# Interleaving attention with the projections in a hybrid decoder block, with the rotary swap moved from TensorE to DMA

## The chip, the cores and the metric

The kernel runs on the eight cores of one Trainium2 chip. Each core computes half of one sequence (2048 tokens of its own, with up to 2048 tokens of history before them) and no core speaks to another. The metric is the device time of the slowest core, in microseconds (us).

Engines: PE is TensorE (PEld its weight loads), ACT is ScalarE, DVE is VectorE, POOL is GpSimd, SP is SyncE. A "q" behind the name means the engine's instruction queue, which also issues DMAs. L306 means line 306 of the program; where a helper function issues every matmul, all matmuls carry one line.

## The reference, cut to what matters

```python
u = rms_norm(h, norm_mix)
q, k, v, z, g_att, g_pool = split(u @ w_in)         # 24 heads of 64; 512 pool channels; 2 gates of 1024
q, k = partial_rope(q), partial_rope(k)             # first 16 dims of each head
att    = dilated_attention(q, k, v)                 # three groups (window, dilation): (128,1) (512,4) (2048,16)
pooled = multiscale_pool(z) @ w_pool_group * scale  # trailing means over 2, 4, 8, 16 tokens, minus the token
merged = sigmoid(g_att) * (att @ w_att_branch) + sigmoid(g_pool) * (pooled @ w_pool_branch)
h = h + merged @ w_out
f = rms_norm(h, norm_ffn)
h = h + (silu(f @ w_ffn_gate) * (f @ w_ffn_up)) @ w_ffn_down
return rms_norm(h, norm_final)
```

Every query sees 129 keys of each group, at distances that are multiples of the dilation. A core works on the heads in four strips; a strip is two heads of each of the three groups. The softmax is taken without subtracting the maximum: two accumulators per head slot collect numerators and denominators of the three groups, and one division per strip ends it ("the norm" of a strip below).

## The kernel before

It is hand-scheduled with explicit semaphores and goes through the stages one by one. x is stored transposed, so tokens are columns. A strip first projects q, k and v of all three groups ("units" of eight matmuls of 512 columns), with a permutation matmul for the rotary partner of each q/k unit:

```python
# one q/k unit
for c in range(8):
    t = mm(psq[:, 0:N], wpv[:, c, wcol:wcol + 128], rhs_fn(c), c == 0, c == 7, after=[t_wp, psq_free[i]])
t_raw = act(qrawv[i], psq, AF.Copy, ...)                 # bf16 copy for the permutation
t_t1  = tt(t1v[i], psq, cosv, ALU.mult, ...)
# one unit later (do_perm)
t_p  = mm(pss, prmv, qrawv[i], True, True, ...)          # 8 rows up, 8 rows down
t_t2 = tt(t2v[i], pss, sinv, ALU.mult, ...)
t_o  = tt(dst, shp(t1v[i]), shp(t2v[i]), ALU.add, ...)
```

Only when all of it is done (`t_Pdone`) does the strip's attention begin, one 128-query block at a time: four score matmuls of 64 rows, an exponential of 512 columns, a mask, four value matmuls. A full barrier stands behind the norm of x, behind the last strip, behind the pooling mixer and behind the gated merge.

```python
for ti, tile in enumerate(tiles):                        # 48 blocks per strip
    ...  mm(ps[:, c0_:c0_ + 128], ktv[...], q, True, True, after=list(sfree[i2]) + t_Pdone)
    t_e = act(ptv[i4], ps2, AF.Exp, after=[t, ptfree[i4]], scale=0.125)
    t_m = tt(ptv[i4], ptv[i4], mv, ALU.mult, after=[t_e, t_msk])
    ...                                                  # value matmuls four blocks later
    # group with dilation 4: output columns slice(r4, 512, 4), that is with a step of 4 in PSUM
P.barrier()                                              # behind the last strip
```

The softmax here doesn't subtract the row's maximum and nothing guards it: scores larger than these inputs give would overflow.

Of the kernel before, what the change touches and what calls it, by code (L numbers as in the profile page):

```python
# [6 lines left out]
F32 = mybir.dt.float32  # L7
# [8 lines left out]
NJ = 22  # L16
EPS = 1e-6
GROUPS = ((128, 1), (512, 4), (2048, 16))
NBLK = (17, 20, 32)
KT_OFF = (0, 2176, 4736)  # L20
VS_OFF = (0, 17 * 192, 37 * 192)

NW = 52512
UT_H, UT_O, ATT = 0, 8192, 16384
CST, MSK, PRM, ONE = 20480, 20608, 21120, 21184
R = 21504
TAB, QT, KT, VS, ACC, WP, PT, QRAW, T12 = R, 25600, 28672, 33088, 39712, 43808, 48416, 49440, 49952
XS, SQ, RS = 25600, 33792, 35840
POOLT, MERGED, TMPB = 29696, 33792, 41984
ACTT, RS2 = 8192, 19456  # L30
FT, WGU, WD, SQ2, SIL, OST = 29696, 33792, 39936, 46080, 48128, 49152

class Tok:
    __slots__ = ("sem", "val")

    def __init__(self, sem, val):
        self.sem, self.val = sem, val

class DSem:
    def __init__(self, sem):  # L40
        self.sem, self.cnt = sem, 0

class Prog:
    ENGS = ("pe", "act", "dve", "pool", "sp")
    CE = ("pe", "act", "dve")

    def __init__(self, nc, es):
        self.nc, self.es = nc, es
        self.ops = {e: [] for e in self.ENGS}
        self.esem = {e: es.enter_context(nc.semaphore("es_" + e)) for e in self.CE}  # L50
        self.ecnt = {e: 0 for e in self.CE}
        self.seen = {e: {} for e in self.ENGS}
        self.nsem = 0
        self.dma_out = []

    def dsem(self):
        self.nsem += 1
        return DSem(self.es.enter_context(self.nc.semaphore(f"ds{self.nsem}")))

    def _waits(self, eng, after):  # L60
        waits = []
        for t in after:
            if t is None:
                continue
            k = id(t.sem)
            if self.seen[eng].get(k, 0) >= t.val:
                continue
            self.seen[eng][k] = t.val
            waits.append((t.sem, t.val))
        return waits  # L70

    def op(self, eng, fn, after=()):
        waits = self._waits(eng, after)
        self.ecnt[eng] += 1
        self.ops[eng].append((waits, fn, (self.esem[eng], 1)))
        return Tok(self.esem[eng], self.ecnt[eng])

    def dma(self, q, out, in_, ds, after=()):
        waits = self._waits(q, after)
        ds.cnt += 16  # L80
        self.ops[q].append((waits, lambda e: e.dma_start(out=out, in_=in_), (ds.sem, 16)))  # L81
        t = Tok(ds.sem, ds.cnt)
        self.dma_out.append(t)
        return t

    def wait(self, eng, after):
        waits = self._waits(eng, after)
        if waits:
            self.ops[eng].append((waits, None, None))

    def barrier(self):
        best = {}
        for t in self.dma_out:
            if id(t.sem) not in best or best[id(t.sem)].val < t.val:
                best[id(t.sem)] = t
        toks = [Tok(self.esem[e], self.ecnt[e]) for e in self.CE if self.ecnt[e] > 0] + list(best.values())
        self.dma_out = []
        for e in self.ENGS:
            self.wait(e, toks)
# [18 lines left out]
def cm_view(ap, g, m):  # L118
    if g == 0:
        return ap[:, 512 * m:512 * m + 512]  # L120
    if g == 1:
        return ap[:, m:2048:4]
    return ap.rearrange("p (i r) -> p r i", r=16)[:, 4 * m:4 * m + 4, :]

def cont_view(ap, g):
    if g == 2:
        return ap.rearrange("p (r i) -> p r i", r=4)
    return ap

class _Stop(Exception):  # L130
    pass

DEBUG = {"stop": None, "dump": (0, 16)}

def build_program():
    nc = bass.Bass("TRN2", target_bir_lowering=False)  # L136
    dr = lambda n, s, k="ExternalInput": nc.dram_tensor(n, list(s), F32, kind=k).ap()
    xT = dr("xT", [D, 4096])
    w_in = dr("w_in", [D, 7168])
    tab = dr("tab", [128, 8192])  # L140
    cst = dr("cst", [128, 128])
    msk = dr("msk", [128, 1024])
    prm = dr("prm", [128, 128])
    wpg = dr("wpg", [128, 512])
    wab = dr("wab", [512, D])
    wpb = dr("wpb", [512, D])
    wout = dr("wout", [D, D])
    wgu = dr("wgu", [D, 2 * DFF])
    wd = dr("wd", [DFF, D])
    oT = dr("oT", [D, NT], "ExternalOutput")  # L150
    if DEBUG["stop"] is not None:
        dbg = dr("dbg", [128, DEBUG["dump"][1]], "ExternalOutput")
    else:
        dbg = None

    with ExitStack() as es:
        P = Prog(nc, es)
        try:
            _body(nc, es, P, locals())
        except _Stop:  # L160
            pass
        P.emit()
    return nc

def _body(nc, es, P, L):
    xT, w_in, tab, cst, msk, prm, wpg, wab, wpb, wout, wgu, wd, oT = [
        L[k] for k in ("xT", "w_in", "tab", "cst", "msk", "prm", "wpg", "wab", "wpb", "wout", "wgu", "wd", "oT")]
    dbg = L["dbg"]

    def chk(name):  # L170
        if DEBUG["stop"] == name:
            P.barrier()
            o, n = DEBUG["dump"]
            t = P.dma("sp", dbg, AR[:, o:o + n], P.dsem())
            P.wait("sp", [t])
            raise _Stop()
    if True:
        AR = es.enter_context(nc.sbuf_tensor("arena", [128, NW], F32))
        PS_ALL = es.enter_context(nc.psum_tensor("ps_all", [128, 4096], F32))
        PSB = [PS_ALL[:, i * 512:(i + 1) * 512] for i in range(8)]  # L180

        def f32(off, n):
            return AR[:, off:off + n]

        def bf(off, n):
            return AR[:, off:off + n // 2].bitcast(BF16)

        def mm(out, lhsT, rhs, start, stop, after=()):
            return P.op("pe", lambda e: e.matmul(out, lhsT=lhsT, rhs=rhs, start=start, stop=stop), after)  # L189

        def act(out, in_, func, after=(), **kw):
            return P.op("act", lambda e: e.activation(out=out, in_=in_, func=func, **kw), after)  # L192

        def tt(out, in0, in1, op, after=()):
            return P.op("dve", lambda e: e.tensor_tensor(out=out, in0=in0, in1=in1, op=op), after)  # L195

        def stt(out, in0, scalar, in1, op0, op1, after=()):
            return P.op("dve", lambda e: e.scalar_tensor_tensor(out=out, in0=in0, scalar=scalar, in1=in1,  # L198
                                                                op0=op0, op1=op1), after)

        uth = bf(UT_H, 8 * 2048).rearrange("p (c t) -> p c t", c=8)
        uto = bf(UT_O, 8 * 2048).rearrange("p (c t) -> p c t", c=8)
        att = bf(ATT, 4 * 2048).rearrange("p (c t) -> p c t", c=4)
        cstv = f32(CST, 128)
        mskv = bf(MSK, 1024)
        prmv = bf(PRM, 128)
        onev = bf(ONE, 128)
        tabv = bf(TAB, 8192)
        tcos_h, tcos_o = tabv[:, 0:2048], tabv[:, 2048:4096]
        tsin_h, tsin_o = tabv[:, 4096:6144], tabv[:, 6144:8192]  # L210

        t_cst = P.dma("sp", cstv, cst, P.dsem())
        t_msk = P.dma("pool", mskv, msk, P.dsem())
        t_prm = P.dma("pool", prmv, prm, P.dsem())
        t_ms1 = P.op("dve", lambda e: e.memset(tabv[:, 0:4096], 1.0))  # L215
        t_ms2 = P.op("dve", lambda e: e.memset(tabv[:, 4096:8192], 0.0))  # L216
        d_tab = P.dsem()
        for p0 in (0, 64):
            t_tab = P.dma("pool", tabv[p0:p0 + 16, :].rearrange("p (a b) -> p a b", b=1024),
                          tab[p0:p0 + 16, :].rearrange("p (a b) -> p a b", b=1024), d_tab, after=[t_ms1, t_ms2])  # L220
        t_one = P.op("dve", lambda e: e.memset(onev, 1.0))
        t_const = [t_cst, t_msk, t_prm, t_tab, t_one]

        wpv = bf(WP, 8 * 1152).rearrange("p (c n) -> p c n", c=8)
        w_inv = w_in.rearrange("(c p) n -> p c n", p=128)
        d_wp = P.dsem()
        t_wp0 = P.dma("pool", wpv, w_inv[:, :, 0:1152], d_wp)

        def rms_stats(src_fn, sqv, rsv, psb, after, rs_after=()):
            ts = []  # L230
            after = list(after) + [Tok(P.esem["pe"], P.ecnt["pe"])]
            for c in range(8):
                ts.append(act(sqv[:, c, :], src_fn(c), AF.Square, after=after))
            t = None
# [709 lines left out]
```

## Time and profile before

Before: 1490.6 us, the median of 15 runs (1488.9 and up; the three runs known when the prediction was made gave 1494.0).

| Stage | from-to, us | length | TensorE busy |
|---|---|---|---|
| norm of x | 0-103 | 103 | 31 |
| strips 0 to 3: projection | four times 92 to 95 | 374 | 354 |
| strips 0 to 3: attention and norm | four times 50 to 52 | 203 | 150 |
| pooling mixer | 680-748 | 68 | 38 |
| gated merge | 748-919 | 171 | 169 |
| output projection | 919-988 | 69 | 62 |
| SwiGLU and the end | 988-1491 | 503 | 471 |

A stage whose two last columns are close is bound by TensorE. The stages where they differ are the ones that the change is after. The lines are in the prediction.

### The profile page before, as it was taken

What the parts mean: (1) busy time and instruction counts of PE and PEld (TensorE: products, weight loads), DVE (VectorE), ACT (ScalarE), POOL (GpSimd) and SP (SyncE); (2) the same over time, 40 slices, a digit from 0 to 9 for tenths busy, and PEclk for the clock granted to TensorE, in tenths of its full rate; (3) what the DMA queues carried; (4) which work ended last, traced back from release to release, by engine and by line L of the source; (5) the groups of instructions that cost most, each with busy time, mean ns of one, the idle gap of its engine ahead of it and who ended that gap; (6) DMA issues with size and microseconds to landing.
All of it is one profiled execution on the core that took longest, in us unless ns stands there. A gap on an engine that the chain in (4) does not pass through costs nothing.

```text
span 1491.1 us, 22251 instructions; the slowest of 8 cores (1474.6 to 1491.1 us)
## 1 busy us (share of the span) xinstructions
PE 1273.9 (85%) x8264; PEld 657.5 (44%) x8264; DVE 701.3 (47%) x1036; ACT 478.7 (32%) x803; POOL 70.5 (5%) x84
## 2 busy tenths in 40 slices
PE   1459977997799889876499997999999998899995
PEld 0026645664466456542144443444444443344442
DVE  3466767775677567766534332541221413221113
ACT  1643355337432733374322221211112214111111
POOL 0000000000000000000101112000010100000000
PEclk9669999998899899997789998999999999999998
DMA  9820040004000300106244243354572555549053
GB/s 189 261 88 2 2 64 2 2 1 65 1 2 2 65 1 1 30 4 225 23 43 42 25 41 35 51 79 63 85 96 39 71 92 116 105 64 133 1 78 113
DMA packets 98967, 89.46 MB, mean 60 GB/s; under 512 B 34960, under 2 KB 81296, under 8 KB 97808
## 3 DMA queue, kind: packets, MB, share of 16 engines
q0 software_dynamic: 84640, 54.43, 27.0%
q1 hardware_dynamic: 14224, 33.62, 7.3%
q8 instruction: 69, 1.13, 0.3%
q14 instruction: 34, 0.28, 0.1%
HBM read 134.09 MB, written 8.39 MB: 96 GB/s over the span
## 4 chain that ended last, share of the span: by engine, by line
PE 77%; DVE 7%; DMA 6%; ACT 5%; issue 3%; DVEq 0%; POOL 0%; SPq 0%; ACTq 0%; POOLq 0%
PE ps_all L189 73%; DVE arena L195 5%; ACT arena L192 5%; DMA arena<-xT 4%; PE ps_all L439 3%; DVE arena L198 2%; PE ps_all L443 2%; DMA oT<-arena 1%; DMA arena<-wpb 1%; DMA arena<-wout 0%; ACT L192 0%; POOL arena L81 0%; DVEq L110 0%; SPq L81 0%; ACTq L110 0%
## 5 line engine op out<-in xcount | busy, mean ns | idle before, releaser
L189 PE MATMUL ps_all<-arena 128*128 128x512 bf16 (+3 forms) x7496 | 1199.8, 322 | 193.7 <-ACT arena L192 101.6
L189 PEld LDWEIGHTS ps_all<-arena 128*128 128x128 bf16 (+1 forms) x7496 | 603.1, 107 | 787.8 <-issue 281.9
L195 DVE TENSOR_TENSOR arena<-ps_all,arena 128x512 f32<-128x512 f32 (+1 forms) x488 | 331.0, 706 | 584.9 <-PE ps_all L189 560.4
L192 ACT ACTIVATE arena<-ps_all 128x512 bf16<-128x512 f32 (+1 forms) x588 | 338.0, 592 | 685.1 <-PE ps_all L189 668.5
L195 DVE TENSOR_TENSOR arena<-arena 128x512 bf16<-128x512 bf16 (+9 forms) x400 | 264.9, 669 | 111.7 <-ACT arena L192 86.5
L192 ACT ACTIVATE arena<-arena 128x512 bf16<-128x512 f32 (+3 forms) x172 | 106.0, 672 | 197.3 <-PE ps_all L189 103.2
L198 DVE SCALAR_TENSOR_TENSOR arena<-arena 128x512 bf16<-128x512 f32 (+1 forms) x144 | 97.7, 739 | 85.8 <-ACT arena L192 73.7
L439 PE MATMUL ps_all<-arena 128*128 128x128 bf16 x384 | 80.2, 261 | 7.4 <-DVE arena L195 7.4
L443 PE MATMUL ps_all<-arena 128*128 128x128 bf16 x384 | 82.0, 266 | 0.0
L81 POOL DMA_DIRECT2D arena<-w_in x21 | 18.6, 892 | 836.7 <-PE ps_all L189 541.8
L439 PEld LDWEIGHTS ps_all<-arena 128*128 128x128 bf16 x384 | 38.5, 109 | 29.4 <-issue 13.0
L443 PEld LDWEIGHTS ps_all<-arena 128*128 128x128 bf16 x384 | 42.5, 111 | 0.0
L192 ACT ACT_TABLE_LOAD x11 | 14.1, 1283 | 88.1 <-PE ps_all L189 64.2
L81 POOL DMA_DIRECT2D arena<-wgu x22 | 19.4, 883 | 324.9 <-PE ps_all L189 324.9
L192 ACT ACTIVATE arena<-ps_all,arena 128x512 f32<-128x512 f32 (+1 forms) x32 | 21.9, 684 | 29.3 <-PE ps_all L189 26.7
L81 POOL DMA_DIRECT2D arena<-wd x8 | 10.8, 1350 | 154.3 <-PE ps_all L189 154.3
L81 POOL DMA_DIRECT2D arena<-wout x8 | 7.0, 919 | 40.0 <-DVE arena L195 40.0
L81 POOL DMA_DIRECT2D arena<-wab x8 | 6.3, 782 | 0.0
L81 POOL DMA_DIRECT2D arena<-wpb x8 | 6.2, 779 | 0.0
L276 DVE MEMSET arena<- 128x4416 bf16 x1 | 3.7, 3738 | 1.5 <-issue 1.5
L215 DVE MEMSET arena<- 128x4096 bf16 x1 | 3.5, 3472 | 2.0 <-PEq L136 2.0
L216 DVE MEMSET arena<- 128x4096 bf16 x1 | 3.5, 3472 | 0.8 <-issue 0.8
(9 smaller groups left out, 3.3 us busy)
## 6 DMA issues: line engine op xcount, KB each, us to landing
arena<-wgu POOLq DMA_DIRECT2D x22, 1024.0 KB, 9.6
arena<-xT SPq DMA_DIRECT2D x8, 2048.0 KB, 15.4
arena<-wd POOLq DMA_DIRECT2D x8, 1408.0 KB, 15.2
arena<-w_in POOLq DMA_DIRECT2D x4, 2304.0 KB, 18.8
arena<-xT SPq DMA_DIRECT2D x8, 1024.0 KB, 16.6
oT<-arena SPq DMA_DIRECT2D x32, 256.0 KB, 2.5
arena<-w_in POOLq DMA_DIRECT2D x16, 256.0 KB, 5.1
arena<-wout POOLq DMA_DIRECT2D x8, 256.0 KB, 10.4
```

Source lines behind the costliest of these rows:

```text
L81: self.ops[q].append((waits, lambda e: e.dma_start(out=out, in_=in_), (ds.sem, 16)))
L189: return P.op("pe", lambda e: e.matmul(out, lhsT=lhsT, rhs=rhs, start=start, stop=stop), after)
L192: return P.op("act", lambda e: e.activation(out=out, in_=in_, func=func, **kw), after)
L195: return P.op("dve", lambda e: e.tensor_tensor(out=out, in0=in0, in1=in1, op=op), after)
L198: return P.op("dve", lambda e: e.scalar_tensor_tensor(out=out, in0=in0, scalar=scalar, in1=in1, op0=op0, op1=op1), after)
L215: t_ms1 = P.op("dve", lambda e: e.memset(tabv[:, 0:4096], 1.0))
L216: t_ms2 = P.op("dve", lambda e: e.memset(tabv[:, 4096:8192], 0.0))
L276: P.op("dve", lambda e: e.memset(vs_all[:, :, 64:128], 1.0))
L439: st=first: en.matmul(o, lhsT=l, rhs=r, start=st, stop=False, skip_group_check=True),
L443: en.matmul(o, lhsT=l, rhs=r, start=False, stop=sp_, skip_group_check=True))
```

## The change

The program was rewritten (1776 lines of diff). Its intent: keep TensorE at work while other engines do attention's softmax, the norm of x and the pooling sums, and take the rotary permutation off TensorE. Cut to its core:

```diff
+# dependencies are now derived from the addresses that each instruction reads and writes; no barriers
-        for tg in range(8):  ...norm of x...
-        P.barrier()
+    for k in range(8):                       # norm of tile k+1 beside the q/k/v units of tile k (strip 0)
+        if k + 1 < 8: norm_sq(k + 1)
+        items = p0_items(k)
+        for _ in range((3, 3, 3, 4, 4, 2, 2, 0)[k]): next(items, None)
+        if k + 1 < 8: norm_rs(k + 1)         # also issues later x loads on the SP queue
+        ...
-            def do_perm(pd): ...permutation matmul, two multiplications, one addition...
+    def rope_out(g):                         # outward leg: six writes to DRAM, one read back, packed on 128 partitions
+        for e in range(2):
+            for k, h0, h1, n in ((0, 0, 0, 16), (1, 0, 8, 8), (1, 8, 0, 8)):
+                P.dma("sp", sav[k][e][h1:h1 + n], qkv[g][64 * e + h0:...], more=not first)
+        return P.dma("sp", xrv[g], sa.rearrange("k p w -> p k w"))
+    def rope_mul(g, i):                      # VectorE; behind the last piece the return leg:
+        ...
+            P.dma("sp", sb, xrv[g][:, 0, :])
+            for e in range(2):
+                P.dma("sp", qkv[g][64 * e:64 * e + 16, :]..., sbv[e])
+        if sp == 0:
+            merge(attn(tiles01()), v2_hist(), T01, 8.0)
+        else:                                # groups 0 and 1 of this strip beside group 2's projection, lead 20%
+            merge(attn(tiles01()), proj(sp, (2,)), T01, proj_cost((2,)), 0.2)
+        if sp < 3:                           # group 2 beside the next strip's groups 0 and 1
+            merge(attn2(sp), proj(sp + 1, (0, 1)), T2, proj_cost((0, 1)), 0.2)
+        else:                                # the last group 2 beside the pooling mixer, no lead
+            merge(attn2(sp), zphase(), T2, 32.0)
```

Below, the way of the rotary rows out to DRAM and back (outward leg, multiply, return leg) is called the detour. `merge` takes instructions from two generators in proportion to their estimated costs; a lead of 20% lets the second run ahead by that share. The exponential and the mask now take two blocks (1024 columns) at once. Weights come in packed layouts and are loaded earlier, and the last SwiGLU product goes token half by token half.

## The prediction

> **What bounds the kernel now.** I read the page's busy shares first, then a table of one stretch per stage (stage borders taken from the gaps in the chain of waits), then the chain itself, then the costs of single forms of instruction.
>
> ```profile
> PE 1273.9 (85%) x8264; PEld 657.5 (44%) x8264; DVE 701.3 (47%) x1036; ACT 478.7 (32%) x803; POOL 70.5 (5%) x84
> ```
>
> TensorE is the bound, but 15% of 1491 us it does nothing, and a busy TensorE need not be at full clock. The stretches show where. Columns: length, then busy us of TensorE, its weight loads, VectorE, ScalarE and GpSimd, then granted clock, DMA share, GB/s.
>
> ```profile
> 0.00:103.00 103.00, 30.97 (x64) 6.61 (x64) 50.19 (x67) 45.70 (x81) 3.35 (x9) 0.76 0.78 195
> 249.00:341.00 92.00, 86.10 (x774) 56.87 (x774) 70.26 (x92) 27.22 (x47) 0.87 (x1) 0.98 0.01 1
> 341.00:391.00 50.00, 39.10 (x432) 23.25 (x432) 28.04 (x58) 37.49 (x61) 0.00 (x0) 0.90 0.32 49
> 680.00:748.00 68.00, 37.90 (x177) 15.73 (x178) 40.98 (x65) 23.82 (x52) 6.50 (x8) 0.80 0.56 142
> 748.00:919.00 171.00, 168.68 (x768) 75.59 (x766) 66.38 (x96) 39.58 (x65) 19.56 (x24) 0.98 0.31 30
> 919.00:988.00 69.00, 61.53 (x272) 27.15 (x272) 31.73 (x48) 12.48 (x21) 8.01 (x10) 0.93 0.43 46
> 988.00:1141.00 153.00, 152.11 (x704) 68.80 (x704) 30.30 (x45) 27.64 (x45) 11.32 (x12) 1.00 0.60 88
> 1228.00:1394.00 166.00, 153.11 (x689) 68.05 (x690) 41.26 (x60) 37.50 (x60) 9.69 (x10) 0.97 0.55 94
> 1475.00:1491.00 16.00, 0.00 (x0) 0.00 (x0) 10.69 (x16) 3.29 (x5) 0.00 (x0) 0.57 0.71 262
> ```
>
> In order: the norm of x (DMA at 78%, TensorE idle 70%); the q/k/v projection of one head strip of four (TensorE full); that strip's attention (TensorE 78%, partly cold, ScalarE 75%); the pooling mixer (44% idle); the gated merge; the output projection; the first SwiGLU half (full); part of the second (a hole of some 13 us); the tail. So 103 + 4 x 50 + 68 us are stages in which TensorE waits for others.
>
> The chain of waits shows what it waits for there:
>
> ```profile
> 1.97 41.20 DMA arena<-xT
> ...
> 244.56 1.92 ACT arena L192
> 249.10 1.77 PE ps_all L189 x12
> 250.89 2.30 DVE arena L195
> ...
> 270.69 65.71 PE ps_all L189 x605
> ...
> 738.41 9.33 DMA arena<-wpb
> 747.87 168.82 PE ps_all L189 x768
> ```
>
> x at the start; ScalarE and VectorE between attention and the next projection; a weight load behind a full barrier before the merge.
>
> Forms of instruction that I use (count, busy us, mean ns):
>
> ```profile
> L192 ACT ACTIVATE arena<-ps_all 128x512 bf16<-128x512 f32 x376 | 220.6, 599 | 295.6 <-PE ps_all L189 293.4 <-PE ps_all L443 0.6
> L195 DVE TENSOR_TENSOR arena<-arena 128x512 bf16<-128x512 bf16 x192 | 79.5, 428 | 60.4 <-ACT arena L192 56.6
> L198 DVE SCALAR_TENSOR_TENSOR arena<-arena 128x512 bf16<-128x512 f32 x112 | 75.7, 738 | 64.1 <-ACT arena L192 62.4
> ```
>
> [...] 704 matmuls in 152.11 us are 216 ns. [...] eight cores run the SwiGLU stage at granted clock 1.00. [...] the trace's 256 KB output stores land after a median 2.5 us.
>
> **The change, part by part.** It is a rewrite, so I count matmuls from both programs. Before: 4456 of 512 columns, 3776 of 128 and 32 of 16, together the page's 8264. The model 0.216 and 0.0557 us each gives 87.6 us for one strip's projection (261 and 561); the trace has 88 us from 249.7 to 337.7, so it holds.
>
> *Removed.* The rotary permutation matmuls, 30 per strip, with their PSUM copies and three VectorE operations. 116 x 0.216 + 4 x 0.0557 = 25 us off TensorE's path. What is left is 4340 x 0.216 + 3776 x 0.0557 = 1148 us: the floor of the new kernel.
>
> *Added for it.* The rotary rows go out to DRAM, come back packed on 128 partitions, are multiplied on VectorE and go back: 12 round trips of four dependent DMA steps, about 11 us each to the multiply and 6 back. They start four to six projection units (some 2 us each) before use, and 20% of the next projection is issued ahead of the next attention. Mostly hidden; I charge 12 us for all.
>
> *Norm merged with strip 0's projection.* TensorE's work there: 64 x 0.216 = 13.8 for the sums of squares, 50.6 for q/k, 53 V blocks x 8 x 0.0557 = 23.6, together 88 us. It can't start before the first two x tiles have landed and been squared (ScalarE handles the next tile's squares before this tile's copies): about 20 us, from 2.1 MB tiles beside the weight loads at the 195 GB/s of this stretch. Some 7 us for cold clock and norm chains: the stage ends near 115. DMA: 16.8 MB of x and 3.8 of the rest at 195 to 260 GB/s ends between 80 and 105, about level. Before, the same work ended at 195.
>
> *Attention interleaved with the next projection.* An attention strip is 384 x 0.0557 = 21.4 us of TensorE, instead of a stage of 50. Per strip two phases follow. Groups 0 and 1 beside the projection of group 2: 14.3 + 20.7 + 14.3 = 49.3 us. Group 2 beside the next strip's groups 0 and 1: 7.1 + 29.8 + 16.5 = 53.4. The sum is 102.7, against 142 now. ScalarE per strip: [...] 30 q/k and 18 V copies x 0.6, norms and accumulator copies about 10, together 78 us; VectorE about 50. Both fit. The first phase of strip 0 has only 21.4 us of TensorE work against 21.4 of ScalarE, so pauses show: 25. The last phase has pooling in place of a projection: TensorE 39 us, but VectorE some 40 (its 41.0 in the old pooling stretch) plus 14 for attention, so 56.
>
> *Merge, output, SwiGLU.* Same matmuls, without barriers and with weights prefetched: 768 x 0.216 + 2 = 168 (171 before); 272 x 0.216 + 1 = 60 (69); 152.5 (153); 368 x 0.216 + 1 = 80.5 (87); second half 720 x 0.216 + 3 for table changes = 158.5 and 80.5 (together 247 with the hole); tail 12, because only 8 of the last 16 scalings come after the last matmul (16).
>
> *Sum.* 115 + 25 + 3 x 53.4 + 3 x 49.3 + 56 + 12 = 516; + 168 + 60 + 152.5 + 80.5 + 158.5 + 80.5 + 12 = 1228. I add 7 for pauses that I cannot place: **1235 us**, 0.83 of before. Of the 259 us gained, about 80 come from the norm, 115 from attention, 12 from pooling, 25 to 30 in the strips' projections (the permutations), the rest from the later stages.
>
> **Rivals.** *The softmax chain stays the bound.* For it: ScalarE is in order, and the projections now have only two PSUM banks, so a copy that stands behind an exponential or a log holds TensorE. Against: 78 of 103 us per strip. If each strip loses 15 us: 1295. *The rotary detour takes the place of the permutation.* A VectorE that waits for a DMA blocks the masks behind it, and so TensorE; 8 phase borders at 12 us give some 1320. For it: four dependent steps; against: the slack above and a DMA share of 0.01 during projections. *x is hidden anyway, or rules the start.* If DMA stays at 195 GB/s and buffers come free late, the first stage ends at 130: 1250. [...] *Better than I think:* no pauses at all, first stage at 105 and pooling at 45: about 1195.
>
> **Range and chances.** The floor of 1148 plus 20 at the start and 12 at the end makes 1180 unreachable. Several small stalls push up, one of the two middle rivals in part adds 30 to 60. So 1200 to 1290 for 8 in 10. Faster by over 2% needs less than 1464, which all rivals reach: 0.96; within 2% 0.03; slower 0.01.
>
> **What would show it.** TensorE's idle share falls from 15% to about 5% and its granted clock rises from 0.94 to 0.98 or more; first dense matmuls near 20 us; phases of 103 us per strip, with ScalarE near 75% busy in them; group 2's last phase longest for VectorE; 152 us SwiGLU halves unchanged. Wrong if TensorE waits over 40 us in all for the DMA of rotary rows or for ScalarE's copies, if the first stage ends after 130, or if the clock in dense stretches is below 0.95.

## The result, and the profile after

The changed kernel takes **1301.7 us** (median of its eight fast runs out of twelve, 1300.0 to 1313.7). Executions in which one die ran at a lower clock are left out of the means. The ratio to the kernel before is 0.8737, 95% interval 0.8718 to 0.8757. Ratios are the mean time of one kernel's fast runs over that of the other's of the same rounds, so not quite the ratio of the medians. The change is much faster, as predicted, but the time lies outside the predicted range (1200 to 1290): 67 us above the point. Against the median of before, 1490.6, the prediction stood for a gain of 256 us, and 189 came.

The page's first line for the changed kernel:

```profile
PE 1201.2 (92%) x8144; PEld 637.7 (49%) x8144; DVE 484.9 (37%) x707; ACT 452.9 (35%) x723; POOL 34.3 (3%) x68
```

TensorE is busy 92% of the span, where the prediction expected 95%. The table of stretches of the changed kernel, cut at its own stage borders (columns as in the prediction: length, busy us of PE, PEld, DVE, ACT, POOL, granted clock, DMA share, GB/s):

```profile
0.00:134.00 134.00, 105.60 (x789) 59.22 (x790) 56.99 (x84) 70.98 (x128) 4.05 (x11) 0.94 0.68 184
134.00:172.00 38.00, 33.65 (x376) 23.46 (x373) 18.64 (x28) 21.94 (x28) 1.59 (x3) 1.00 0.59 132
172.00:223.70 51.70, 45.12 (x528) 31.29 (x529) 25.46 (x34) 27.26 (x44) 1.06 (x2) 0.99 0.42 86
223.70:341.20 117.50, 110.74 (x1177) 74.93 (x1178) 46.17 (x66) 58.90 (x89) 1.59 (x3) 0.96 0.33 70
341.20:458.60 117.40, 115.27 (x1201) 77.19 (x1202) 47.91 (x68) 60.41 (x91) 1.59 (x3) 0.98 0.31 66
458.60:519.00 60.40, 48.85 (x577) 36.68 (x575) 19.35 (x29) 26.93 (x37) 0.53 (x1) 0.92 0.30 66
519.00:583.70 64.70, 46.26 (x303) 21.13 (x304) 49.13 (x77) 32.24 (x61) 0.00 (x0) 0.89 0.10 33
583.70:1299.30 715.60, 695.74 (x3203) 313.75 (x3201) 221.21 (x324) 154.26 (x249) 23.85 (x45) 0.99 0.39 80
```

In order: the norm of x with strip 0's projection; strip 0, groups 0 and 1; its group 2; strip 1; strip 2; strip 3, groups 0 and 1; the last group 2 with pooling; all the rest. Against the prediction's 115, 25, 53.4, 102.7, 102.7, 49.3 and 56, everything before 583.7 us is too long, by 80 us in all (12 of these had been charged to the detour as a lump, 7 to pauses); the rest took 716 where 712 was predicted. So nearly all of the miss lies in the first 584 us.

What holds TensorE at the end of a strip can be read in the timeline of the changed kernel around 195 to 228 us. Each row has start, length, engine, instruction, and in brackets the idle time before it and what ended it:

```profile
203.02 4.62 SPq L224 DMA_DIRECT2D sa<-arena  x6
210.67 0.39 SPq L224 DMA_DIRECT2D arena<-sa  x1
218.00 7.23 DVE L313 TENSOR_TENSOR arena<-arena 128x576 f32<-128x576 bf16 x10 [6.07 <-DMA arena<-sa]
220.98 2.07 ACT L310 ACTIVATE arena<-arena 64x512 f32<-64x512 f32 x3 [4.88 <-DVE arena L313]
223.68 4.85 PE L306 MATMUL ps_all<-arena 128*128 128x512 bf16 x11 [4.76 <-ACT arena L310]
```

Read from the bottom: TensorE stood still for 4.8 us and was released by ScalarE. ScalarE had waited 4.9 us for VectorE, since a logarithm of the strip's norm stood in its queue ahead of the copies that TensorE needed. VectorE had waited 6.1 us for the DMA that brings the rotary rows back (`sa`), since the rotary multiply stood in its queue ahead of the norm. That read was issued at 210.7, because the six writes ahead of it were only issued from 203.0 on. The chain of waits names what held those: the first half of the return leg of the group before, 4.4 us of DMA from 197.7 on, for whose landing the same SP queue waited. Four queues in order, each holding the next.

The same queue delays the last x tile in the first stage. The SP queue's rows of the changed kernel, 80 to 135 us:

```profile
87.78 4.42 SPq L224 DMA_DIRECT2D sa<-arena  x6
94.93 0.39 SPq L224 DMA_DIRECT2D arena<-sa  x1
95.42 4.97 SPq L224 DMA_DIRECT2D sa<-arena  x6
103.08 0.39 SPq L224 DMA_DIRECT2D arena<-sa  x1
103.57 0.41 SPq L224 DMA_DIRECT2D arena<-xT  x1
```

The buffer of the last x tile was free at 95.8 us (end of the scaling of the tile that had it), but its load was issued at 103.6, behind two outward legs that wait for their own writes.

### The profile page after: what moved, and what is told of

Its sections match the earlier page's. It is cut to its first block, busy times and chain, and to the rows that moved or that the text cites. A ratio compares the mean times of both kernels' runs of the same rounds, so it can differ in the third digit from the quotient of the medians.

```text
span 1299.3 us, 20667 instructions; the slowest of 8 cores (1284.8 to 1299.3 us)
## 1 busy us (share of the span) xinstructions
PE 1201.2 (92%) x8144; PEld 637.7 (49%) x8144; DVE 484.9 (37%) x707; ACT 452.9 (35%) x723; POOL 34.3 (3%) x68
## 4 chain that ended last, share of the span: by engine, by line
PE 76%; DMA 9%; DVE 8%; ACT 3%; issue 3%; SPq 2%; DVEq 0%; ACTq 0%
PE ps_all L306 76%; DVE arena L313 5%; ACT arena L310 3%; DVE arena L317 3%; DMA arena<-xT 2%; SPq L224 2%; DMA sb<-arena 2%; DMA arena<-sa 2%; DMA arena<-sb 1%; DMA sa<-arena 1%; DMA oT<-arena 1%; ACT L310 0%; DVE arena L595 0%; DVEq L242 0%; DVEq L234 0%
## 5 line engine op out<-in xcount | busy, mean ns | idle before, releaser
L306 PE MATMUL ps_all<-arena 128*128 128x512 bf16 (+2 forms) x8144 | 1201.2, 312 | 88.3 <-ACT arena L310 47.3
L306 PEld LDWEIGHTS ps_all<-arena 128*128 128x128 bf16 (+1 forms) x8144 | 637.7, 107 | 651.6 <-issue 158.5
L310 ACT ACTIVATE arena<-ps_all 128x512 f32<-128x512 f32 (+2 forms) x476 | 308.8, 672 | 590.5 <-PE ps_all L306 578.6
L313 DVE TENSOR_TENSOR arena<-ps_all,arena 128x512 f32<-128x512 f32 (+1 forms) x248 | 179.8, 736 | 461.9 <-PE ps_all L306 452.3
L313 DVE TENSOR_TENSOR arena<-arena 128x1024 bf16<-128x1024 bf16 (+12 forms) x292 | 195.3, 684 | 230.2 <-ACT arena L310 204.5
L310 ACT ACTIVATE arena<-arena 128x512 bf16<-128x512 f32 (+3 forms) x204 | 113.5, 599 | 117.8 <-DVE arena L313 98.6
L224 POOL DMA_DIRECT2D arena<-wgu x22 | 11.7, 531 | 330.7 <-PE ps_all L306 267.3
L595 DVE COPY arena<-ps_all 128x512 f32<-128x512 f32 x16 | 11.0, 685 | 9.4 <-PE ps_all L306 9.4
L224 POOL DMA_DIRECT2D arena<-wq x12 | 6.5, 544 | 263.1 <-PE ps_all L306 245.7
L224 POOL DMA_DIRECT2D arena<-wd x8 | 4.2, 532 | 172.6 <-PE ps_all L306 172.4
```

What stands on the lines that cost most here:

```text
L224: self.ops[q].append((waits, lambda e: e.dma_start(out=out, in_=in_), (sem, 16)))
L306: return P.op("pe", lambda e: e.matmul(out, lhsT=lhsT, rhs=rhs, start=start, stop=stop, **kw), [lhsT, rhs], [out])
L310: return P.op("act", lambda e: e.activation(out=out, in_=in_, func=func, **kw), rd, [out])
L313: return P.op("dve", lambda e: e.tensor_tensor(out=out, in0=in0, in1=in1, op=op), [in0, in1], [out])
L595: en.tensor_copy(out=o, in_=i), [PSB[OB[e]]], [accv[e][:, 512 * m:512 * m + 512]])
```

## The experiments

The calls ran on different chips. To set runs of different calls side by side, "scaled" below is the median of the fast runs times 1490.6 over the median of the fast runs of the kernel before in the same call (1492.2, 1494.8, 1494.2 and 1490.8). The changed kernel stands at 1301.7. The scaled figures are good to a few us (e16, the same kernel on another chip, comes to -0.7; the kernel before itself ran from 1488.5 to 1507.6 in its fast runs), so differences of 5 us and less decide nothing here.

| Run | fast runs | median | scaled | to the changed kernel |
|---|---|---|---|---|
| e1 no detour (wrong result) | 4 of 4 | 1264.4 | 1263.0 | -38.7 |
| e2 return leg on another queue | 3 of 4 | 1287.5 | 1286.1 | -15.6 |
| e3 last x tile on another queue | 2 of 4 | 1297.4 | 1296.1 | -5.6 |
| e4 V copies on VectorE | 3 of 5 | 1310.5 | 1309.2 | +7.5 |
| e5 lead for pooling | 4 of 4 | 1293.8 | 1290.2 | -11.5 |
| e6 dense output (wrong result) | 4 of 4 | 1294.4 | 1290.7 | -11.0 |
| e7 in turn | 3 of 4 | 1388.2 | 1384.3 | +82.6 |
| e9 dense output, stepped input | 3 of 4 | 1308.7 | 1305.0 | +3.3 |
| e8 all three | 3 of 4 | 1289.6 | 1286.4 | -15.3 |
| e11 output in runs of 32 (wrong result) | 3 of 4 | 1297.9 | 1294.7 | -7.0 |
| e12 one sum (wrong result) | 2 of 4 | 1290.6 | 1287.5 | -14.2 |
| e13 all three and dense | 4 of 5 | 1293.2 | 1290.0 | -11.7 |
| e14 all three, queue put right | 4 of 4 | 1272.9 | 1272.7 | -29.0 |
| e15 e14 and dense, kept in order | 4 of 4 | 1283.8 | 1283.7 | -18.0 |
| e16 the changed kernel again | 4 of 4 | 1301.2 | 1301.0 | -0.7 |

**e1: the rotary detour taken out.**

```diff
     def rope_out(g):
+        return None
     def rope_mul(g, i):
+        return
-    P.wait("pool", [rope_out(2)])
```

> The rotary detour taken out whole: no write of the rotary rows to DRAM, no multiply, no read back (the result is wrong on purpose). Theory D, the detour holds TensorE: the waits that end with a DMA of rotary rows or with the multiply behind it add up to some 40 us (in the profile of the changed kernel: 5 to 6 at the end of each strip plus 2 to 3 of cold clock after it, 12 before the last group 2, about 8 in the start through the x load that stands behind the detour in the issue queue), so about 1262 us. Rival M, the matmuls themselves are dearer than the model and ScalarE's copies hold them: less than 10 us gained, 1292 or more.

1263.8 to 1265.6 us. Theory D stands: the detour costs 39 us, where the prediction had 12 for it and 7 more for pauses that it could not place. The stretches of this kernel, at its own borders (strip 0's groups 0 and 1; strip 1; the last group 2 with pooling):

```profile
126.00:152.60 26.60, 23.81 (x346) 19.48 (x346) 12.47 (x18) 19.03 (x22) 0.53 (x1) 1.00 0.62 98
208.30:317.60 109.30, 107.87 (x1180) 74.35 (x1178) 32.60 (x44) 58.73 (x88) 1.59 (x3) 1.00 0.12 23
481.00:546.60 65.60, 47.75 (x314) 21.83 (x314) 51.84 (x80) 34.95 (x66) 0.75 (x2) 0.92 0.19 46
```

Strip 1 is 8 us shorter than with the detour, and its clock is 1.00 where it was 0.96: behind the stop of 4.8 us TensorE ran for some us at half clock (from 223.7 to 228.5 us in the changed kernel the granted clock was 0.50; above, the 11 matmuls behind the stop take 4.85 us, 0.44 each and not 0.216). But 109.3 is still 6.6 above the predicted 102.7, and the pooling phase is 65.6 where 56 was predicted. The detour is the largest part of the miss, not all of it. Between the two traces (spans 1299.3 and 1262.5 us) TensorE stands idle 28.7 us less and is busy 8.1 us less: I take the second figure for what the slower clock behind the stops cost, about.

**e2: the return leg on the GpSimd queue.**

```diff
-            P.dma("sp", sb, xrv[g][:, 0, :])
+            P.dma("pool", sb, xrv[g][:, 0, :])
-                P.dma("sp", qkv[g][64 * e:64 * e + 16, :]..., sbv[e])
+                P.dma("pool", qkv[g][64 * e:64 * e + 16, :]..., sbv[e])
```

> Only the return leg of the detour (packed rows to DRAM, DRAM to the q/k rows) issued from the GpSimd queue instead of the SyncE queue, so that the next group's outward leg does not wait behind it. Result correct. Theory Q, the order of the one queue makes most of the wait: the stalls of 5 to 6 us at the ends of strips go, about 15 to 19 us gained, 1283 to 1287. Rival L, it is the length of the round trip itself: unchanged within 4 us.

15.6 us gained, with the same DMAs and bytes: theory Q stands. What held TensorE at the ends of the strips was the order of the SP queue. The idle times of some 5 us at those places are gone from its timeline; both legs are now issued at the same time, and TensorE runs on behind its 1.1 us:

```profile
200.58 5.39 SPq L224 DMA_DIRECT2D sa<-arena  x6
200.58 0.56 POOL L224 DMA_DIRECT2D sb<-arena  x1 [31.54 <-DVE arena L313]
210.51 79.00 PE L306 MATMUL ps_all<-arena 128*128 128x128 bf16 x872 [1.12 <-ACT arena L310]
```

A faster path is not the reason: the second half of the return leg follows the first by 5.5 us here (200.6 to 206.0) and by 4.5 before (197.7 to 202.2). The wait at the last border, before the last group 2, stays (6.8 us). What the move saved is waiting in a queue: the return leg waits for its own first half (4.4 us from 197.7 us on in the changed kernel), and on the SP queue the six writes of the next outward leg stood behind it until 203.0.

**e3: the last x tile on the GpSimd queue.**

```diff
-        P.dma("sp", f32(XS[k], 4096), T["xT"][TILES[k]])
+        P.dma("pool" if k == 7 else "sp", f32(XS[k], 4096), T["xT"][TILES[k]])
```

> Only the load of the last x tile issued from the GpSimd queue. It is issued at 103.6 us now, though its buffer is free at 95.8, because the SyncE queue waits for the detour's writes. Theory Q: the first stage ends 7 to 8 us earlier, about 1294 us. Rival: the load is hidden or limited by bandwidth, within 3 us of 1302.

Only two of its four runs were fast (1297.2 and 1297.7), so there is no interval. In its trace, strip 0's attention begins at 130.8 us and not at 134.6. So about half of the delay in the queue came through; the rest was hidden by other work. The direction is clear, the size is not better than a few us.

**e4: the V copies on VectorE.**

```diff
-        act(dst, ps[:, 0:nb * 128]..., AF.Copy)
+        P.op("dve", lambda en: en.tensor_copy(out=dst, in_=sv), [sv], [dst])
```

> The 18 V copies per strip moved from ScalarE to VectorE. Rival S, ScalarE in order (exponentials ahead of PSUM copies) holds TensorE: 15 us or more gained, below 1288. Theory D: ScalarE is only 55% busy in the strips, so within 5 us of 1302, with VectorE now also blocking the copies while it waits for the detour, so if anything slower.

7.5 us slower: 18 copies per strip less on ScalarE gained nothing, and on VectorE they stood behind the rotary multiply. Its profile fell in a slow run, but on a core of the undisturbed die (core 5, clock 0.975) VectorE waits 8.0 us for the rotary rows before 218.8 us, and TensorE 7.2 us for a copy behind them. By itself e4 doesn't clear ScalarE, since the copies met a new wait. e1 does: with all copies still on ScalarE, TensorE is busy 107.9 of the 109.3 us of strip 1.

**e5: a lead for the pooling mixer.**

```diff
-            merge(attn2(sp), zphase(), T2, 32.0)
+            merge(attn2(sp), zphase(), T2, 32.0, 0.2)
```

> One argument changed: the pooling mixer gets the same lead of 20% over the last attention that the projections have. Theory D: the 9 to 12 us in which TensorE waits for the last rows of the detour before the last group 2 are then filled with pooling work, 8 to 10 us gained, about 1292 us. Rival V, the last phase is bound by VectorE's sums alone, whatever the order: within 4 us of 1302.

11.5 us gained with one argument, a little more than the 8 to 10 expected. In the changed kernel TensorE waits 9.2 us from 510 us on for the last rows of the detour:

```profile
519.16 0.26 PE L306 MATMUL ps_all<-arena 64*128 64x128 bf16 x1 [9.18 <-DMA arena<-sb]
```

The reason is that the pooling phase alone had no lead: nothing independent stood ahead of group 2 in TensorE's queue. With three pooling units ahead the wait is filled: 1.6 us of it is left in e5's trace.

**e6, e9, e11: the stepped output.** Group 1 (dilation 4) writes its output with a step of 4 in PSUM, before and after the change. e6 only makes it dense:

```diff
-  slice(r4, 512, 4), False, r4 == 3
+  slice(r4 * 128, r4 * 128 + 128), False, r4 == 3
```

> The second attention group writes its PSUM output columns next to each other and not with a step of 4 (columns in the wrong order, so the result is wrong on purpose). In the profile a matmul of 128 columns with that step takes 105 ns and one without 56. Theory P: 64 such matmuls per strip x 50 ns, in the three strips that TensorE bounds: 10 us gained, at most 13 with the first strip, about 1290 us. Rival: they lie beside waits, within 3 us of 1302.

11 us gained, so theory P stands: the stepped output costs what the spacing of the matmuls says. It could have been seen before. These are value matmuls of the kernel *before*, at full clock, first of a group 1 block, then of a group 0 block (the granted clock is 1.00 from 351.2 us on):

```profile
351.53 0.31 PE L443 MATMUL ps_all<-arena 128*128 128x128 bf16 x1
351.64 0.31 PE L439 MATMUL ps_all<-arena 128*128 128x128 bf16 x1
351.75 0.31 PE L443 MATMUL ps_all<-arena 128*128 128x128 bf16 x1
...
352.28 0.22 PE L443 MATMUL ps_all<-arena 128*128 128x128 bf16 x1
352.33 0.22 PE L439 MATMUL ps_all<-arena 128*128 128x128 bf16 x1
352.39 0.22 PE L443 MATMUL ps_all<-arena 128*128 128x128 bf16 x1
```

The starts are 110 ns apart in the first three and 50 to 60 in the last three. I took the slow ones for half clock; they are the stepped ones, a factor of two at the same granted clock. The changed kernel shows the same: 105 ns stepped and 57 dense, both at clock 1.00 (eight matmuls from 241.4 and from 238.8 us on).

e9 makes it dense and right, by reading group 0's probabilities with a step of 4:

```diff
+                        if g == 0:
+                            o = PSB[OB[e]].rearrange("p (r i) -> p r i", r=4)[:, :, k4:k4 + 32]
+                            p0, p1 = [p.rearrange("p (i r) -> p r i", r=4) for p in (p0, p1)]
```

> The same as with the dense output, but right: the first group's probabilities are read with a step of 4 so that its output too lies in the second group's order, in runs of 32 columns, and the copy from PSUM puts the order right. If a stepped moving operand costs nothing: as with the dense output, about 1290 us. If it costs what a stepped output does: no gain, 1302 us or more.

No gain: in its trace the first group's value matmuls start 113 ns apart, and the second group's 57. The cost moved from one group to the other. e11 tells which half of that edit costs, by reading the probabilities in storage order with the same output:

```diff
-                            p0, p1 = [p.rearrange("p (i r) -> p r i", r=4) for p in (p0, p1)]
+                            p0, p1 = [p.rearrange("p (r i) -> p r i", r=4) for p in (p0, p1)]
```

> As the right dense version (which gained nothing: its first-group matmuls took 113 ns), but the probabilities are read in storage order; only the output goes in runs of 32 columns (wrong result on purpose). If the stepped read of the moving operand was what cost: 56 ns per matmul and about 1291 us, as with the dense output. If the runs of 32 in the output cost: still 105 ns or more, 1302 us or more.

All value matmuls start 57 ns apart. So an output in runs of 32 columns cost no more than a dense one (57 ns), and the stepped read of the moving operand is what doubled the time in e9 (113 ns). The kernel gained 7 us, less than e6, and lay between the two expectations; its copies out of PSUM are stepped like those of e13 (1058 ns each on VectorE there, 685 in the changed kernel). That these cost the difference is not tested alone.

**e7: one after the other.**

```diff
-            merge(attn(tiles01()), proj(sp, (2,)), T01, proj_cost((2,)), 0.2)
+            run(proj(sp, (2,)))
+            run(attn(tiles01()))
-            merge(attn2(sp), proj(sp + 1, (0, 1)), T2, proj_cost((0, 1)), 0.2)
+            run(attn2(sp))
+            run(proj(sp + 1, (0, 1)))
```

> Attention and projection no longer interleaved: in each phase one runs after the other (the start and the pooling phase stay as they are). Theory I, interleaving is the main gain of the strips: attention alone is bound by exponentials and latency, 27 us for groups 0 and 1 (as in the first strip) and some 19 for group 2 with its norms, so about 10 us more per phase in six phases, less the detour's waits, which the projections then cover: 1320 to 1340 us. Rival: most of the gain came from leaving out barriers and the permutation, 1300 or less.

83 us slower, where 20 to 40 were expected. Interleaving is worth more than theory I gave it. Stretches of this kernel (two projections' worth of TensorE work; strip 1's groups 0 and 1 alone; its group 2 with the norm alone):

```profile
206.00:288.00 82.00, 81.11 (x785) 54.58 (x785) 9.74 (x14) 26.22 (x46) 1.05 (x2) 0.98 0.39 81
288.00:318.00 30.00, 20.36 (x268) 15.04 (x261) 17.97 (x27) 18.69 (x22) 0.53 (x1) 0.89 0.25 54
318.00:351.00 33.00, 16.48 (x134) 9.41 (x135) 18.37 (x24) 15.86 (x22) 0.00 (x0) 0.71 0.00 1
```

Groups 0 and 1 alone take 30 us, near the 27 expected; group 2 and its norm take 33, not 19. In the latter no engine is busy for much more than half of the time, and the clock is 0.71, where it was 0.98 in the projections before: it is a chain of matmul, exponential, mask, matmul, sum, logarithm, and TensorE ran it at the lower clock. Together that is 63 us for a strip's attention alone, more than the 50 to 52 of the kernel before; so the 83 us are not what interleaving gained over that kernel.

**e12: one window sum.**

```diff
-                for lvl in range(gz + 1):
+                for lvl in range(1):
```

> In the pooling mixer one window sum per tile and not one to four: 24 sums of 0.71 us fewer on VectorE, all else kept (wrong result on purpose). Theory V, the last phase is bound by VectorE, with attention's masks and sums standing in its queue behind the pooling sums: 12 to 17 us gained, 1285 to 1290 us. Rival: its length comes from ScalarE's copies and the two PSUM banks: under 5 us gained.

14.2 us gained for 17 us of sums taken away: VectorE does hold the last phase. The other part of theory V, attention's own sums standing behind the pooling sums, is argued from rows such as a value matmul at 538 us that waited 3.3 us for VectorE.

**e8 and e14: the three repairs together.** e8 is e2, e3 and e5 in one kernel.

> Return leg and last x tile on the GpSimd queue, and the lead for the pooling mixer, together; result correct. If the three waits are separate their gains add: 13 + 4 + 8, about 1277 us, leaving some 12 us to the kernel without the detour (1264). If they hide each other: 1284 or more.

15.3 us gained, where the parts give 15.6 + 5.6 + 11.5 = 32.7. Its own profile says where the rest went (first a row of TensorE, then, from the GpSimd queue's timeline, two rows):

```profile
506.16 0.58 PE L306 MATMUL ps_all<-arena 128*128 128x16 bf16 x16 [14.23 <-DMA arena<-wz]
```

```profile
493.58 1.02 POOL L224 DMA_DIRECT2D arena<-sb  x2 [2.74 <-DMA sb<-arena]
494.59 0.57 POOL L224 DMA_DIRECT2D arena<-wz  x1
```

The pooling weights (`wz`) are loaded from the GpSimd queue, and now stood there behind the return leg of group 2 (e2's trace already had 4.5 us of this wait). The mistake of the changed kernel, made again in another queue. e14 leaves group 2's return leg on the SP queue:

```diff
+            rq = "sp" if g == 2 else "pool"
-            P.dma("pool", sb, xrv[g][:, 0, :])
+            P.dma(rq, sb, xrv[g][:, 0, :])
```

> The three repairs together, but the return leg of group 2 left on the SyncE queue, so that the pooling weights don't wait behind it. Result correct. Theory Q: the 14 us wait for the pooling weights goes and the gains add, about 25 us under the changed kernel of the same call, 1277 us. If the repairs hide each other for another reason: 1285 or more.

1270.8 to 1273.6 us, ratio to the kernel before 0.8533 (0.8517 to 0.8550): 29 of the 32.7 us. The gains nearly add once no load stands behind a wait that isn't its own. Of the 39 us that the detour cost, 29 can be had back with the detour in place, although e5's lead also fills time that isn't the detour's. What holds the last 10 us was not tested. **e14 beats both kernels**, with a correct result.

> The changed kernel once more, unaltered, for a comparison on one chip: 1300 to 1305 us in its fast state.

e16, in the same call as e14, gives 1301.0 to 1303.0 us, ratio 0.8731: the 28 us between them hold on one chip.

**e13 and e15: dense output as well.** e13 is e8 with group 0's queries stored in the second group's order by the copy behind the projection, so that no matmul is stepped:

```diff
+            if typ == 0:
+                dst = dst.rearrange("p (k r i) -> p k r i", k=4, r=4)
+                sv = sv.rearrange("p (k i r) -> p k r i", k=4, r=4)
```

> All three changes, and the second group's output dense with the queries of the first group stored in the second's order already by the copy after the projection (tables permuted to match, mask read with a step on VectorE); result correct. If runs of 32 in the output cost nothing: some 10 us under the version with three, about 1267 us. If they cost as a step does: no better than it, 1277 to 1285.

No better than e8 (both have the wait for `wz`, here 13.7 us). By the trace, what was taken from TensorE went to VectorE: the copy of the accumulators out of PSUM, now stepped, takes 1058 ns on VectorE in e13, and 685 in the changed kernel, and TensorE waits for it (12.8 us in all, 1.8 in e8), because those PSUM banks have no second copy. e15 is e14 with dense output and the accumulators kept in that order:

```diff
-  tt(att[0:64, sp, cs], accv[0][0:64, cs], nt[0:64, :], ALU.mult)
+  tt(att[0:64, sp, cs].rearrange("p (i r) -> p r i", r=4), accv[0][0:64, cs].rearrange("p (r i) -> p r i", r=4), ...)
```

> The same, and the output of the second group dense, with the accumulators kept in that order, so that the copies from PSUM need no step; the order is put right in the last multiplication of the norm. Result correct. 10 us under the version with three repairs if VectorE's stepped mask and stepped last multiplication stay hidden, about 1268 us; if they hold TensorE as the stepped copies did, no gain over it.

11 us slower than e14. These copies are at 686 ns again, but the last multiplication of the norm now has a step (e15's group of that form):

```profile
L313 DVE TENSOR_TENSOR arena<-arena 64x512 bf16<-64x512 f32 x32 | 42.2, 1319 | 12.7 <-ACT arena L310 12.2
```

It takes 1319 ns a piece, and 683 in the changed kernel. The stepped mask is dearer too: the mean over all masks rises from 692 to 868 ns. That these are what holds TensorE is argued from its waits for ScalarE (39.6 us in all, 30.2 in e14), not tested alone. None of the three right versions (e9, e13, e15) had the dense output for nothing.

## Why the prediction was wrong

The mechanism was right and sizes were off. The detour (12 + 7 predicted, 39 measured) is the term that failed most; the rest is spread over three others. The kernel without the detour (e1) lets the terms be read one by one, from its stage borders at 126, 152.6, 208.3, 317.6, 426.8, 481 and 546.6 us:

| Term of the sum | predicted | measured | off by | settled by |
|---|---|---|---|---|
| detour and unplaced pauses | 12 + 7 | 39 | +20 | e1, e2, e14 |
| start to the first attention | 115 | 126 | +11 | trace |
| strips, up to the last group 2 | 333 | 355 | +22 | e6 for 11 of it, trace |
| last group 2 with pooling | 56 | 66 | +10 | e12 |
| merge to the end | 712 | 716 | +4 | trace |

The sum is 67, the difference of 1301.7 and 1235. (333 is 25 + 2 x 102.7 + 53.4 + 49.3; 355 is 481 - 126.)

- *"Mostly hidden; I charge 12 us for all."* This step failed. The prediction named the right rival ("the rotary detour takes the place of the permutation", with a VectorE that blocks the masks behind it) and took it for unlikely, because each round trip had slack before its use. The slack was counted per round trip. What was not counted is that the legs of different groups share one in-order queue, so that the outward leg of group 1 is issued only after the first half of group 0's return leg has landed, and that the lead which covers the other borders is missing at the last one. e2 and e5 show both. The legs were also longer than charged: on the chain of waits, the outward leg takes 12 to 17 us to the multiply (203.0 to 218.0, 318.1 to 335.5, 435.7 to 447.7), not the 11 that I had estimated, and the return leg 8 to 12 (164.0 to 172.0, 453.7 to 465.4, 507.8 to 520.0), not the estimated 6. Two of the prediction's own signs of being wrong came: TensorE waits over 40 us (12.9 for the rotary rows and 47.3 for ScalarE, 17.1 of these before the first matmul), and the first stage ends after 130 (at 134.6).
- *The start.* The term allowed 20 us of waiting, 7 of slow pace and 88 of work. In e1's first 126 us TensorE is idle for 23.6 and busy for 102.4, though its 770 matmuls there are worth 90 at the prediction's prices: about 12 us were lost to pace. One place is the first tile, whose 111 matmuls take 19.3 us, where the 104 of each of the next two tiles take 12.5. The end of the stage is the norm chain of the last x tile, with nothing left to put beside it: TensorE waits for its scalings one by one between 117 and 122 us (123 and 128 in the changed kernel). In the changed kernel the x tile itself came 8 us late through the queue, of which e3 got about half back; these 8 us belong to the detour's 39 and not to this term.
- *102.7 us per strip.* TensorE's count was right; the price of 55.7 ns for every matmul of 128 columns was not. Dense ones do start 56 ns apart (changed kernel, 236.3 to 236.7 us), but a third of the value matmuls, those of group 1, took about twice that (105 ns). The prediction checked its prices on the projection only, where no output is stepped. Beyond the 11 us of e6, some 11 us in these phases stay without an experiment. The single starts in e1's trace place part of them: in strip 1 (6.6 us too long) the stepped value matmuls are some 3.4 us dearer than priced, about 220 matmuls of 128 columns start 62 ns apart and not 56 (1.5 us), and TensorE waits 1.4 us. The pauses at each change between 64-row and 128-row matmuls (about 0.1 us each way) are not the cause: the score matmuls of a strip's two heads start in pairs, 3 ns apart, and so take half of their price, which pays for the pauses.
- *Pooling, 56 us.* VectorE was named as its bound, and e12 confirms it. The term added busy times (40 + 14) and took VectorE for full, but with the two chains in turn in its one queue it also waited: it was busy 49 of 64.7 us.
- *What held.* Merge, output projection and SwiGLU within 4 us (the 3 us for table changes are an estimate; the traces show 11 table loads on ScalarE in either kernel, 1.28 us each); attention no longer a stage; ScalarE not the bound (e1); full granted clock in dense stretches (1.00 on all eight cores in the merge of the changed kernel's profiled run). Whether attention brought the 115 us ascribed to it is not shown: e7 undoes the interleaving alone, for 83 us, with an attention that differs from that of the kernel before.
- *A slip in the sums.* ScalarE's 78 us per strip do not come out. An exponential of 1024 columns took 1.02 us in the changed kernel (128x1024, 96 of them); 24 of these, 48 copies x 0.6 (599 ns in the kernel before) and 10 make 63 us. The changed kernel's two full strips show 59 and 60, half of their length and not 75%. The slip does not enter the 1235.
- *The range.* It ran to 1290 and had the detour's rival "in part" at plus 30 to 60. With the floor at 1180 known, most of the uncertainty was above the point, and the range should have gone to about 1320.

## What to carry to other kernels

When work moves from a compute engine to DMA, count the queue that issues it: here a DMA that waited 4.4 us for data held the six writes behind it in that queue, and through the queues of VectorE (6.1 us) and ScalarE (4.9 us) the wait reached matmuls that have nothing to do with it (4.8 us); an estimate of slack per round trip misses this. Give each chain of dependent DMAs a queue of its own, or place it where nothing urgent follows, and look again after each move, since the wait can turn up in the next queue (14.2 us in e8). And price matmuls from the trace by their access pattern, not only by their columns (128 columns took 105 ns with a step of 4 in the output, 113 with one in the moving operand, 56 with neither).
